# A hybrid encoder block on one core: the plan of its long convolution rearranged, and a second buffer for turned chunks

## The chip, the cores and the metric

The kernel runs on one core of a Trainium2 chip (one launch, one program). The metric is the device time of one execution in microseconds. Times are medians of several executions; the profile is of one more execution of the same program.

## What is computed

One block for 256 tokens of width 2048, in float32:

```python
proj = h @ w_in
q, k, v, r, af, ab, hy_u, gate_logits = split(proj)
y_gla = gla(q, k, v, r, af, ab)              # gated linear attention, both directions
uc = short_conv(hy_u)                        # 3 taps and a bias per channel
z, x1, x2 = split(uc, 3)
for o, gate in enumerate((x1, x2)):          # a long convolution by FFT, twice
    z = gate * (irfft(rfft(z, 2 * L) * filt_f[:, o])[:L] + skip[o] * z)
g = sigmoid(gate_logits)
merged = g[0] * (y_gla @ w_gla_o) + g[1] * (z @ w_hy_o)
h = layernorm(ALPHA * h + merged @ w_out)
ff = relu(h @ w_ff1) ** 2 @ w_ff2
out = layernorm(ALPHA * h + ff)
```

## The kernel before

**Weights.** All large weights lie in HBM as blocks of 128 x 2048 float32 values (1 MB). `fetch` (L100) loads one block through SyncE's queue into one of three `raw` buffers and splits each half of it into a high and a low part: ScalarE casts the half to `whi` (L92), and VectorE subtracts (`wlo`, L93). There are three buffers of each, so a cast can begin only when TensorE has finished with the half three before it. `token_group` (L242) multiplies four blocks with both token halves: `token_half` (L224) does 12 matmuls of 512 columns per half block, three for each pair of a block row and a token half (L233 to L235). Its two results lie in two of the four main PSUM buffers; they must be read out before the next group but one begins. Two blocks are always loaded ahead of the one that is being multiplied.

**The stretch around the change.** For each of four units of 512 channels, four token groups run one after the other: the three inputs v, x1 and x2 of the convolution (tiles `uv`, `ux`, L942), and one group of the attention's output projection (`go`, L903). Beside them the rest of the convolution has to be done for the unit. This work is put between the weight halves by a planner. `work(at, cost, fn)` (L119) files a step with a due time; `on_time` (L123) does the same for a step that must stay in program order. `fill` (L126) is called once after each half block, which is one tick. It adds 1.75 us to a budget (of which at most 0.875 us is carried over) and takes steps strictly by due time until the first one is not yet due or costs more than is left:

```python
budget[0] = min(budget[0], PACE / 2) + PACE
while filling:
    e = min(filling, key=lambda e: e[:2])
    if not every and (e[0] > tick[0] or e[2] > budget[0]):
        break
```

A unit has 32 ticks; its start is the tick at which its v group has been filed. `keep_in_program_order` fixes the order of the steps that it is given among each other; where the rest goes on its engine is chosen when the program is built.

**The steps of one unit.** `short_conv` (L765) makes each of the three inputs: six products of a PSUM result with a row of taps (L773: two centre taps into the input's tile `cv` or `cx`, two "past" taps and two "ahead" taps into side tiles, the upper half of `conv_sb` or `shift`), the bias (L777), and then `shift` (L779): four accumulating DMAs in GpSimd's queue (L787) that add the side tiles into the input, moved by one token, and the load of the next input's taps in SyncE's queue (L760). Then, twice (order 0 with v and x1, order 1 with the result and x2):

- `load`: the filter's spectrum from HBM into `Tl` through GpSimd's queue (L802); one buffer
- `input`: ScalarE casts the whole input to `zh` (L809); `low`: VectorE's remainder `zl` (L813)
- `fwd`: 12 matmuls of the forward transform into four PSUM buffers of the side pool, which has four (`Ze`, `Zo`), and two copies to `pb` (L824)
- `sum`, `mul`, `join`, `fold`, `split`: VectorE (L830, L842, L846, L853, L863), with a ScalarE cast in each split (L862)
- `inv`: 12 matmuls into two side PSUM buffers (`yp`); `gate`: two VectorE products with x1 or x2 (L876)

After order 1, `turn`: `hy_turn` (L878) transposes a chunk of 256 channels on TensorE into a side PSUM buffer (`yT`), ScalarE copies it to `yo` (L889), and a step filed two ticks later stores `yo` to HBM through GpSimd's queue (`yd`, L893). The tile `yo` has one buffer, the tag `sum` of the pool `base`. Two chunks come from each unit; the last two of the eight are split directly and not stored. After the last unit, while four groups of gate logits (`g`) run, the six stored chunks are loaded again (L955), and the projection `ho` reads all eight.

The due times stand in `PLAN` (L908), counted from the unit's start, and in the loop at L940: v's taps at 0, x1's at 8, x2's at 16. Most of a unit's order 1 falls into the ticks of the next unit.

Of the kernel before, what the change touches and what calls it, by code (L numbers as in the profile page):

```python
# [9 lines left out]
F32 = mybir.dt.float32  # L10
# [6 lines left out]
P = 128  # L17
D = 2048
L = 256
# [30 lines left out]
def block_kernel(  # L50
# [28 lines left out]
    base = ctx.enter_context(tc.tile_pool(name="base", bufs=1))  # L79
# [8 lines left out]
    def psum_side(name):  # L88
        return sdp.tile([P, 512], F32, tag="sd", name=name)

    def split_hi_lo(hi, lo, src):
        return (nc.scalar.copy(hi, src),  # L92
                nc.vector.tensor_tensor(lo, src, hi.bitcast(F32), op=ALU.subtract))  # L93
# [25 lines left out]
    def work(at, cost, fn):  # L119
        clock[1] += 1  # L120
        filling.append((at, clock[1], cost, fn))

    def on_time(at, cost, fn):  # L123
        work(at, cost, lambda: tc.keep_in_program_order(fn()))
# [12 lines left out]
    def weight_half(n, h):  # L137
        return (wp.tile([P, D // 2], F32R, tag="whi", bufs=3, name=f"whi{n}_{h}"),
                wp.tile([P, D // 2], F32R, tag="wlo", bufs=3, name=f"wlo{n}_{h}"))
# [149 lines left out]
    with tc.tile_pool(name="xp", bufs=1) as xp, tc.tile_pool(name="xq", bufs=1) as xq:  # L289
# [25 lines left out]
        for i in range(3):  # L315
            t = weight_half(-1, i)
# [194 lines left out]
    for i in range(2 * NCH):  # L511
        c, o = divmod(i, 2)
        n = 4 + (i * 21) // 15
# [236 lines left out]
    hp = hstk.enter_context(tc.tile_pool(name="hp", bufs=1))  # L750
# [8 lines left out]
    def load_taps(i):  # L759
        return nc.sync.dma_start(conv_sb[:, 0:2].rearrange("p a b -> p (a b)"),  # L760
                                 conv_rows[i:i + 1, :].broadcast_to([P, 2048]))
# [3 lines left out]
    def short_conv(at, pss, i, tag, name):  # L765
        past, ahead = shifted[i % 2][:, 0:NT], shifted[i % 2][:, NT:]

        def place():
            cst[tag, i // 3] = hp.tile([P, NT, 512], F32, tag=tag, name=name)

        def tap(j, tb):
            y = cst[tag, i // 3]
            return TT((past, y, ahead)[j][:, tb], pss[tb], taps[:, j], op=ALU.mult)  # L773

        def bias():
            y = cst[tag, i // 3]
            return TT(y, y, taps[:, 3:4].broadcast_to([P, NT, 512]), op=ALU.add)  # L777

        def shift():  # L779
            y = cst[tag, i // 3]  # L780
            for dst, src in (
                (y[:, 1], past[:, 0]),
                (y[1:P, 0], past[0:P - 1, 1]),
                (y[:, 0], ahead[:, 1]),
                (y[0:P - 1, 1], ahead[1:P, 0]),
            ):
                nc.gpsimd.dma_start(dst, src, accum_op=ALU.add)  # L787
            if i + 1 < 12:
                tc.keep_in_program_order(load_taps(i + 1))

        work(at, 0.0, place)
        for n, (j, tb) in enumerate((j, tb) for j in (1, 0, 2) for tb in range(NT)):
            on_time(at + 0.4 * n, 0.68, lambda j=j, tb=tb: tap(j, tb))
        on_time(at + 2.4, 1.2, bias)
        work(at + 2.4, 0.0, shift)

    def halves_of(ap):
# [2 lines left out]
    def hy_load(s, o):  # L800
        t = hp.tile([P, 2, 1024], F32, tag="Tl", name=f"Tl{s}{o}")
        nc.gpsimd.dma_start(t, T_dram[(s, o)].rearrange("p r h s c -> p r (h s c)"))  # L802
        cst[("T", s, o)] = t

    def hy_input(s, o):
        src = cst.pop(("v", s)) if o == 0 else cst[("x1", s)]
        z = tuple(hp.tile([P, NT, 512], F32R, tag=t, name=f"{t}{s}{o}") for t in ("zh", "zl"))
        cst[("z", s, o)] = z + (src,)
        tc.keep_in_program_order(nc.scalar.copy(z[0], src))  # L809

    def hy_low(s, o):
        zh, zl, src = cst[("z", s, o)]
        return TT(zl, src, zh.bitcast(F32), op=ALU.subtract)  # L813

    def hy_fwd(s, o):
        zh, zl, _ = cst.pop(("z", s, o))
        x = hp.tile([P, 2, 2, 2, CW], F32, tag="X", name=f"X{s}{o}")
        b = hp.tile([P, 2, 1024], F32, tag="pb", name=f"pb{s}{o}")
        odds = []
        for ri in range(2):  # L820
            even, odd = psum_side(f"Ze{s}{o}{ri}"), psum_side(f"Zo{s}{o}{ri}")
            for ps, i in ((even, 0), (odd, 1)):
                mm3(ps, dfth[:, 2 * i + ri], dftl[:, 2 * i + ri], zh[:, i], zl[:, i], True, True, hold=True)
            nc.scalar.copy(b[:, ri, 0:512], even)  # L824
            odds.append(odd)
        cst[("X", s, o)] = (x, b, odds)

    def hy_sum(s, o, ri, k):
        x, b, odds = cst[("X", s, o)]
        return TT(x[:, ri, :, k], halves_of(b[:, ri, 0:512]), halves_of(odds[ri]), op=(ALU.add, ALU.subtract)[k])  # L830

    def hy_mul(s, o, ri, k):
        x, b, _ = cst[("X", s, o)]
        t = cst[("T", s, o)]
        x = x.rearrange("p r h k c -> p r (h k c)")
        if ri == 0:
            if k == 0:
                cst[("a", s, o)] = hp.tile([P, 2, 1024], F32, tag="pa", name=f"pa{s}{o}")
            b = cst[("a", s, o)]
        else:  # L840
            x = x[:, ::-1]
        return TT(b[:, k], x[:, k], t[:, ri], op=ALU.mult)  # L842
# [31 lines left out]
    def hy_gate(s, o, i):  # L874
        g = cst[(("x1", "x2")[o], s)]
        return TT(g[:, i], cst.pop(("py", s, o, i)), g[:, i], op=ALU.mult)  # L876

    def hy_turn(c, zf):  # L878
        def run():
            pt = psum_side(f"yT{c}")  # L880
            for cc in range(2):
                for tb in range(NT):
                    nc.tensor.transpose(pt[:, cc * L + tb * P:cc * L + (tb + 1) * P], zf[:, tb, cc * P:(cc + 1) * P], ident)
            pt = pt.rearrange("p (a b) -> p a b", a=2)
            if c >= NCH - 2:
                split_hi_lo(yhT[:, 2 * c:2 * c + 2, 0], yhT[:, 2 * c:2 * c + 2, 1], pt)
                return
            yo = base.tile([P, 2, L], F32, tag="sum", name=f"yo{c}")
            nc.scalar.copy(yo, pt)  # L889

            def keep():
                yd = drp.tile([P, 2, L], F32, tag=f"yd{c}", name=f"yd{c}")
                nc.gpsimd.dma_start(yd, yo)  # L893
                yh_dram[c] = yd
            work(tick[0] + 2, 0.0, keep)
        return run
# [3 lines left out]
    def gla_o_group(at):  # L900
# [4 lines left out]
        for tb in range(NT):  # L905
            on_time(at, 0.68, lambda tb=tb: TT(mg[:, tb], mg[:, tb], pss[tb], op=ALU.mult))

    PLAN = (  # L908
        dict(load=3, input=9, low=9.5, fwd=10.4, sum=11.5, mul=12, join=15, fold=17.6, split=19.5, inv=20.5, gate=22),
        dict(load=16.5, input=22.5, low=23, fwd=26, sum=26.5, mul=28, join=30.5, fold=35, split=36.5, inv=37,  # L910
             gate=41, turn=43),
    )

    def unit_steps(at, s):
        for o, plan in enumerate(PLAN):
            t = {k: at + v for k, v in plan.items()}
            work(t["load"], 0.0, lambda o=o: hy_load(s, o))
            work(t["input"], 0.0, lambda o=o: hy_input(s, o))
            on_time(t["low"], 1.2, lambda o=o: hy_low(s, o))
            work(t["fwd"], 0.0, lambda o=o: hy_fwd(s, o))  # L920
            for ri in range(2):
                for k in range(2):
                    on_time(t["sum"], 0.68, lambda o=o, ri=ri, k=k: hy_sum(s, o, ri, k))
            for ri in range(2):
                for k in range(2):
                    on_time(t["mul"], 1.2, lambda o=o, ri=ri, k=k: hy_mul(s, o, ri, k))
            for step, fn in (("join", hy_join), ("fold", hy_fold), ("split", hy_split)):
                for k in range(2):
                    on_time(t[step], 1.2, lambda o=o, k=k, fn=fn: fn(s, o, k))
            work(t["inv"], 0.0, lambda o=o: hy_inv(s, o))  # L930
            for i in range(2):
                on_time(t["gate"], 0.68, lambda o=o, i=i: hy_gate(s, o, i))
            if o:
                for i in range(2):
                    work(t["turn"] + 2 * i, 0.0, lambda i=i: hy_turn(
                        2 * s + i, cst[("x2", s)][:, :, i * CW:(i + 1) * CW])())

    load_taps(0)
    paced[0] = True
    for s in range(NCH // 2):  # L940
        for n, (k, d) in {"v": (0, 0), "x1": (1, 8), "x2": (2, 16)}.items():
            pss = token_group(xT, f"u{n}{s}")  # L942
            if k == 0:
                t0 = tick[0]
                unit_steps(t0, s)
            short_conv(t0 + d, pss, 3 * s + k, n, f"c{n}{s}")
        gla_o_group(t0 + 24)
# [615 lines left out]
    with tc.high_priority(), tc.issue_after(done.ins):  # L1563
# [3 lines left out]
        y, t, v, rs = (ep.tile([P, 1], F32, tag=f"fin{i}", name=f"fin{i}") for i in range(4))  # L1567
# [160 lines left out]
```

## Time and profile before

| | us |
|---|---|
| median of 3 runs | 1802.42 |
| lowest and highest of them | 1802.08, 1803.63 |
| the profiled execution | 1799.02 |
| its span, first to last instruction | 1797.1 |
| VectorE busy in the span | 1460.3 |
| ScalarE busy in the span | 1047.8 |
| first matmul of `uv` to first matmul of `g` after the units | 429.8 to 839.2 |

In the rows of the profile, PE is TensorE, PEld its weight load, DVE VectorE, ACT ScalarE, POOL GpSimd and SP SyncE. A row in order of time gives the start in us from the span's start, the duration in us, the engine, the line, the operation, the tile written and the tiles read, and the count; in brackets stands how long the engine was idle before it and what ended that. A row of waits gives the waiting engine, tile and line, what it waited for, and then the sum in us, the number of waits and the longest. In a row of stretches, the number in brackets counts the instructions that were at work in the stretch; the granted clock, the share of the DMA engines and their GB/s follow.

### The profile page before, as it was taken

The page shows a single profiled execution, that of the slowest core. Times are in us where ns is not written, and L with a number is a line of the kernel's source. Part 1 is how long each engine was busy: PE and PEld are TensorE (multiplying, and loading weights), DVE is VectorE, ACT ScalarE, POOL GpSimd, SP SyncE. Part 2 cuts the span into 40 slices and gives each one's busy share as a digit, 9 for nine tenths or more (in the row PEclk, how much of TensorE's full clock was granted, in tenths as well). Part 3 has the DMA queues.
Part 4 walks back from the last instruction along what each step waited for, and adds up shares of the span by engine and source line. Part 5 has one row for each costly group of instructions (what it writes and reads, how often), then busy time and mean ns, then how long its engine had stood idle before and what let it go on. Part 6 is the DMA issues. An engine that isn't in the chain of part 4 may idle for free.

```text
span 1797.1 us, 23574 instructions
## 1 busy us (share of the span) xinstructions
PE 1775.9 (99%) x8739; PEld 1497.7 (83%) x8739; DVE 1460.3 (81%) x1899; ACT 1047.8 (58%) x1446; POOL 186.7 (10%) x243
## 2 busy tenths in 40 slices
PE   9999999999999999999999999999999999999998
PEld 7888888888788788787888889988888888888886
DVE  6689887785588788787855557789999999999998
ACT  6587876785344343443544435666666666666663
POOL 1001111000011101111000000011111111111110
PEclk9999999999999999999999999999999999999999
DMA  8677888545688778778655574588888888887864
GB/s 329 224 265 264 278 256 260 172 156 210 212 280 253 232 233 254 229 256 244 221 181 193 212 289 173 200 257 245 254 264 244 243 273 244 267 252 242 262 216 166
DMA packets 87315, 427.13 MB, mean 238 GB/s; under 512 B 9816, under 2 KB 14312, under 8 KB 45600
## 3 DMA queue, kind: packets, MB, share of 16 engines
q1 hardware_dynamic: 47664, 336.35, 51.1%
q0 software_dynamic: 30560, 67.38, 18.1%
q10 hardware_dynamic: 8976, 21.89, 3.4%
q8 instruction: 68, 1.11, 0.2%
q14 instruction: 47, 0.39, 0.1%
HBM read 382.12 MB, written 12.06 MB: 219 GB/s over the span
## 4 chain that ended last, share of the span: by engine, by line
PE 50%; DVE 3%; DMA 0%; issue 0%; ACT 0%; DVEq 0%
PE f L176 12%; PE f L180 6%; PE w L1360 5%; PE w L1359 5%; PE w L1361 5%; PE g L233 2%; PE g L234 2%; PE ho L234 2%; PE ho L233 2%; PE g L235 2%; PE ho L235 2%; PE wo L234 1%; PE wo L235 1%; PE wo L233 1%; PE f L209 1%; DVE zr L1217 1%
## 5 line engine op out<-in xcount | busy, mean ns | idle before, releaser
L93 DVE TENSOR_TENSOR wlo<-raw,whi 128x1024 fp32r<-128x1024 f32 x360 | 438.9, 1223 | 198.5 <-ACT whi L92 195.8
L92 ACT CAST whi<-raw 128x1024 fp32r<-128x1024 f32 x360 | 376.9, 1054 | 366.9 <-PE ux L235 93.1
L176 PE MATMUL f<-hT,whi 128*128 128x512 f32 x984 | 243.9, 391 | 0.0
L176 PEld LDWEIGHTS f<-hT,whi 128*128 128x128 f32 x984 | 180.8, 188 | 34.9
L1217 DVE TENSOR_TENSOR wlo<-fraw,whi 128x1024 fp32r<-128x1024 f32 x112 | 136.9, 1222 | 14.2 <-ACT whi L1220 10.9
L180 PEld LDWEIGHTS f<-hT,wlo 128*128 128x128 f32 x984 | 126.2, 191 | 4.8
L180 PE MATMUL f<-hT,wlo 128*128 128x256 f32 x984 | 127.7, 283 | 0.0
L1220 ACT CAST whi<-ring 128x1024 fp32r<-128x1024 f32 x56 | 59.0, 1054 | 114.3 <-DVE ring L1217 114.3
L1280 POOL DMA_DIRECT2D ring<-wblk x56 | 48.6, 868 | 728.7 <-DVE ring L1217 722.3
L1220 ACT CAST whi<-fraw 128x1024 fp32r<-128x1024 f32 x112 | 117.7, 1051 | 0.0
L1220 ACT CAST b_h<-ring 128x1024 fp32r<-128x1024 f32 x112 | 87.9, 834 | 22.7 <-PE w L1361 21.1
L234 PE MATMUL ux<-wlo,xT 128*128 128x512 f32 x256 | 100.5, 392 | 0.5 <-DVE wlo L93 0.5
L234 PE MATMUL g<-wlo,xT 128*128 128x512 f32 x256 | 100.3, 392 | 0.0
L235 PE MATMUL ux<-whi,xT 128*128 128x512 f32 x256 | 100.3, 392 | 0.0
L235 PE MATMUL g<-whi,xT 128*128 128x512 f32 x256 | 100.0, 391 | 0.0
L233 PE MATMUL g<-whi,xT 128*128 128x512 f32 x256 | 92.5, 391 | 0.6 <-DVE shift L773 0.6
L233 PE MATMUL ux<-whi,xT 128*128 128x512 f32 x256 | 90.7, 390 | 2.4 <-ACT whi L92 2.4
L1217 DVE TENSOR_TENSOR ring<-ring 128x512 f32<-128x512 f32 x112 | 77.2, 689 | 1.9
L1217 DVE TENSOR_TENSOR b_l<-ring,b_h 128x1024 fp32r<-128x1024 f32 x56 | 68.4, 1221 | 8.6 <-ACT b_h L1220 8.5
L1217 DVE TENSOR_TENSOR wlo<-ring,whi 128x1024 fp32r<-128x1024 f32 x56 | 68.6, 1225 | 2.8 <-ACT whi L1220 1.0
L1217 DVE TENSOR_TENSOR fa<-ring,fa 128x1024 fp32r<-128x1024 f32 x56 | 68.3, 1219 | 0.0
L1281 POOL DMA_DIRECT2D ring<-ring x56 | 65.7, 1174 | 0.1
(529 smaller groups left out, 4268.0 us busy)
## 6 DMA issues: line engine op xcount, KB each, us to landing
raw<-wblk SPq DMA_DIRECT2D x188, 1024.0 KB, 5.0
fraw<-wblk SPq DMA_DIRECT2D x56, 1024.0 KB, 4.9
ring<-wblk SPq DMA_DIRECT2D x56, 1024.0 KB, 6.9
ring<-wblk POOLq DMA_DIRECT2D x56, 256.0 KB, 4.4
ring<-ring POOLq DMA_DIRECT2D x56, 256.0 KB, 5.1
conv_sb<-conv_rows SPq DMA_DIRECT2D x12, 1024.0 KB, 5.8
w<-w4s ACTq DMA_DIRECT2D x16, 512.0 KB, 5.2
Td<-T POOLq DMA_DIRECT2D x32, 256.0 KB, 4.8
```

Source lines behind the costliest of these rows:

```text
L92: return (nc.scalar.copy(hi, src), nc.vector.tensor_tensor(lo, src, hi.bitcast(F32), op=ALU.subtract))
L93: nc.vector.tensor_tensor(lo, src, hi.bitcast(F32), op=ALU.subtract))
L176: MM(ps[:, :, ts], hi[:, js], act[:, kt, :, ts], start=(kt == 0 and opens), stop=(kt == KT - 1))
L180: MM(ps[:, 0, ts], lo[:, js], act[:, kt, 0, ts], start=False, stop=False)
L233: order(MM(pss[tb], sh, wh, start=(kt == ends[0]), stop=False))
L234: order(MM(pss[tb], sh, wl, start=False, stop=False))
L235: order(MM(pss[tb], sl, wh, start=False, stop=(kt == ends[1])))
L1217: return pin(nc.vector.tensor_tensor(dst, a, b, op=op))
L1220: return pin(nc.scalar.copy(hi, src))
L1359: pin(MM(ps, sh, wh, start=(p == begin), stop=False))
L1360: MM(ps, sh, wl, start=False, stop=False)
L1361: pin(MM(ps, sl, wh, start=False, stop=(p == end - 1)))
```

## The change

Four things change. In `short_conv` the bias is filed at 0.6 behind the two centre taps, ahead of the four outer ones, instead of at 2.4 behind all six. In `PLAN` nearly all due times move: the input cast of order 0 from 9 to 11.6, its remainder and transform after it, the products spread by 0.7 a step, joins from 15 to 19, and in order 1 the load from 16.5 to 20 and the input cast from 22.5 to 24.6. The third input's taps are due at 16.2 instead of 16, which is now ahead of the first order's joins. The copies of turned chunks alternate between the pool `base` and the pool `hp`, so there are two buffers, and the second turn is due one tick behind the first and not two.

```diff
@@ short_conv
         for n, (j, tb) in enumerate((j, tb) for j in (1, 0, 2) for tb in range(NT)):
+            if n == 2:
+                on_time(at + 0.6, 1.2, bias)
             on_time(at + 0.4 * n, 0.68, lambda j=j, tb=tb: tap(j, tb))
-        on_time(at + 2.4, 1.2, bias)
         work(at + 2.4, 0.0, shift)
@@ hy_turn
-            yo = base.tile([P, 2, L], F32, tag="sum", name=f"yo{c}")
+            yo = (hp if c % 2 else base).tile([P, 2, L], F32, tag="sum", name=f"yo{c}")
@@ PLAN
-        dict(load=3, input=9, low=9.5, fwd=10.4, sum=11.5, mul=12, join=15, fold=17.6, split=19.5, inv=20.5, gate=22),
-        dict(load=16.5, input=22.5, low=23, fwd=26, sum=26.5, mul=28, join=30.5, fold=35, split=36.5, inv=37,
-             gate=41, turn=43),
+        dict(load=3, input=11.6, low=12, fwd=12.2, sum=13.6, mul=14, join=19, fold=20, split=21, inv=21.5, gate=24.2),
+        dict(load=20, input=24.6, low=25, fwd=25.5, sum=28, mul=29.5, join=35, fold=36.5, split=38, inv=38.5,
+             gate=41, turn=42.5),
@@ unit_steps
-                    on_time(t["mul"], 1.2, lambda o=o, ri=ri, k=k: hy_mul(s, o, ri, k))
+                    on_time(t["mul"] + 1.4 * ri + 0.7 * k, 1.2, lambda o=o, ri=ri, k=k: hy_mul(s, o, ri, k))
-                    work(t["turn"] + 2 * i, 0.0, lambda i=i: hy_turn(
+                    work(t["turn"] + i, 0.0, lambda i=i: hy_turn(
                         2 * s + i, cst[("x2", s)][:, :, i * CW:(i + 1) * CW])())
@@ the loop over units
-        for n, (k, d) in {"v": (0, 0), "x1": (1, 8), "x2": (2, 16)}.items():
+        for n, (k, d) in {"v": (0, 0), "x1": (1, 8), "x2": (2, 16.2)}.items():
```

## The prediction

> **What bounds the kernel now.** The page first: which engine is full, and how full.
>
> ```profile
> span 1797.1 us, 23574 instructions
> PE 1775.9 (99%) x8739; PEld 1497.7 (83%) x8739; DVE 1460.3 (81%) x1899; ACT 1047.8 (58%) x1446; POOL 186.7 (10%) x243
> ```
>
> TensorE has work at nearly every moment of the 1797.1 us, so an edit elsewhere can gain only what TensorE loses now. Second, the waits of 400 to 960 us, the stretch that holds the part of the program which the plan orders:
>
> ```profile
> ACT yo L889 <- DMA yd<-yo: 24.6, 3, 8.7
> ...
> DVE cx L876 <- PE yp L374: 17.5, 8, 4.2
> ...
> PE go L233 <- ACT whi L92: 8.2, 3, 3.3
> ...
> PE ux L233 <- ACT whi L92: 2.4, 1, 2.4
> ...
> PE g L233 <- DVE shift L773: 0.6, 1, 0.6
> ...
> PE uv L233 <- DVE conv_sb L773: 0.3, 1, 0.3
> ```
>
> Four times TensorE waits for a weight cast (whi): three times in a go group, once in a ux group. Behind that stand two waits of ScalarE for a DMA: the copy of a turned chunk (yo) waits for the store of the chunk before it, and the input cast (zh) waits for the adding DMAs of the convolution. Third, ScalarE in order of time, at the first and the second of the four places, with one undisturbed weight cast ahead of them:
>
> ```profile
> 457.39 1.05 ACT L92 CAST whi<-raw 128x1024 fp32r<-128x1024 f32 x1 [1.67 <-PE ux L235]
> ...
> 487.63 1.04 ACT L809 CAST zh<-cv 128x1024 fp32r<-128x1024 f32 x1 [7.42 <-DMA cv<-conv_sb]
> 488.58 1.99 ACT L92 CAST whi<-raw 128x1024 fp32r<-128x1024 f32 x2
> ...
> 617.22 0.58 ACT L889 COPY yo<-yT 128x512 f32<-128x512 f32 x1 [8.71 <-DMA yd<-yo]
> ```
>
> The weight casts queue behind the waiting instruction and come out in a row afterwards (x2). Undisturbed, one comes each 1.05 + 1.67 = 2.72 us: that is a tick of the plan. Fourth, TensorE around the first place and the last:
>
> ```profile
> 486.65 0.39 PE L234 MATMUL ux<-wlo,xT 128*128 128x512 f32 x1
> 486.88 0.39 PE L235 MATMUL ux<-whi,xT 128*128 128x512 f32 x1
> 489.67 0.73 PE L233 MATMUL ux<-whi,xT 128*128 128x512 f32 x2 [2.40 <-ACT whi L92]
> 490.93 0.79 PE L234 MATMUL ux<-wlo,xT 128*128 128x512 f32 x1 [0.53 <-DVE wlo L93]
> 491.52 0.63 PE L235 MATMUL ux<-whi,xT 128*128 128x512 f32 x1
> 491.95 0.63 PE L234 MATMUL ux<-wlo,xT 128*128 128x512 f32 x1
> ...
> 828.01 0.78 PE L233 MATMUL go<-whi,yg 128*128 128x512 f32 x2 [1.82 <-ACT whi L92]
> 829.27 0.80 PE L234 MATMUL go<-wlo,yg 128*128 128x512 f32 x1 [0.48 <-DVE wlo L93]
> 829.86 0.63 PE L235 MATMUL go<-whi,yg 128*128 128x512 f32 x1
> ...
> 839.17 0.47 PE L233 MATMUL g<-whi,xT 128*128 128x512 f32 x1 [0.64 <-DVE shift L773]
> ```
>
> Starts lie 0.23 us apart before the wait (486.65, 486.88) and 0.43 us apart after it (491.52, 491.95). So a wait costs more than its length: matmuls run slower for a few us behind it. The whole price is therefore read from counts. A 20 us stretch without a wait, then one around each of the four places:
>
> ```profile
> core 0: us, PE busy (x), PEclk, DMA share, GB/s
> 540.00:560.00 20.00, 20.00 (x90) 1.00 0.72 244
> 480.00:500.00 20.00, 17.07 (x69) 0.91 0.56 172
> 612.00:632.00 20.00, 15.89 (x61) 0.91 0.65 215
> 718.00:738.00 20.00, 16.07 (x61) 0.91 0.64 214
> 822.00:842.00 20.00, 17.06 (x67) 0.91 0.68 216
> ```
>
> 90 matmuls fit where nothing waits; 21, 29, 29 and 23 are missing at the four places, and the granted clock is 0.91 in each. A matmul of this shape takes 0.227 us (starts of 486.65 to 486.88, and 20 us over the 88 or so that start in the first stretch), so the places lose 4.8 + 6.6 + 6.6 + 5.2 = 23.1 us. The last three stretches also hold the small waits for a released PSUM buffer (0.64 and its like, rows g and uv). No other stretch of this part of the program holds a listed wait: 23.1 us is all that the plan can give.
>
> **The change part by part.**
>
> *Bias ahead of the outer taps.* VectorE does the same six products and one sum per input; only their order changes, so its work costs nothing more. The adding DMAs go out earlier. Before:
>
> ```profile
> 459.62 1.28 DVE L773 TENSOR_TENSOR cv<-uv,conv_sb 128x512 f32<-128x512 f32 x2
> 460.81 0.68 DVE L773 TENSOR_TENSOR conv_sb<-uv,conv_sb 128x512 f32<-128x512 f32 x1
> ...
> 462.54 1.88 DVE L773 TENSOR_TENSOR conv_sb<-uv,conv_sb 128x512 f32<-128x512 f32 x3
> 464.34 1.22 DVE L93 TENSOR_TENSOR wlo<-raw,whi 128x1024 fp32r<-128x1024 f32 x1
> 465.47 1.23 DVE L777 TENSOR_TENSOR cv<-cv,conv_sb 128x1024 f32<-128x1024 f32 x1
> ...
> 467.01 1.82 POOL L787 DMA_DIRECT2D cv<-conv_sb  x2 [35.77 <-DVE cv L777]
> ...
> 479.95 0.88 POOL L787 DMA_DIRECT2D cv<-conv_sb  x1 [2.77 <-DMA cv<-conv_sb]
> ```
>
> The first add waits for the bias, the last of the seven steps, which ends at 466.7. In the new order it needs two centre taps (1.2 us, 459.62 to 460.81), the bias and one weight remainder (1.13 each, 464.34 to 465.47) and two "past" taps (1.2): 459.62 + 4.7 = 464.3, so the chain starts 2.4 us earlier. It took from 467.01 to the release of zh at 487.63, 20.6 us; shifted it lands at 485.2.
>
> *Input cast from 9 to 11.6 (first order).* Going through the planner's rule tick by tick (strictly by due time, 1.75 us of budget per half block), the cast sits behind weight cast 9 of the unit before the change and behind weight cast 12 after it. Weight cast 1 is the row of 457.39, so weight cast 12 starts at 457.39 + 11 x 2.72 = 487.3 and the input cast at 488.3: 3.1 us after the adds have landed. The 7.42 us wait goes, and with it the 4.8 us of the first place. If the cover of 3.1 us were missed, more slack follows: weight cast 10 was due at 481.9, started at 488.58, 6.7 us late, and TensorE waited 2.40 of that, so 4.3 us of ScalarE's lateness cost nothing. What is late next: in the later units the cast is at tick 12 instead of 10 and has two ticks (5.4 us) and the earlier adds for itself.
>
> *Two buffers for turned chunks, and turns one tick apart.* Before, the planner puts the first copy at tick 12 of the next unit; its store and the second copy, both held up behind the products of the second frequency step, come together at tick 17, and the one buffer makes the second copy wait for the store to land (8.71 us, three times). After, both turns sit at tick 12, both stores at tick 15, and each copy's buffer was last used a unit, 32 ticks, earlier. The three waits go: 6.6 + 6.6 + 5.2 us. At tick 12 ScalarE then has a weight cast, two copies and the input cast, 1.05 + 2 x 0.58 + 1.04 = 3.25 us in 2.72: 0.5 us late, inside the 4.3.
>
> *Third input's taps ahead of joins and folds.* They sit at ticks 18 to 20 instead of 19 to 22, before TensorE needs their PSUM buffers at the next group but one. The waits of 0.3 to 0.6 us go; they are in the 23.1 already.
>
> *Later sums, products, joins, folds, splits and gates.* The same instructions. The first order's gates fall at tick 26 (24 and 25 before), the second order's at 10 and 11 of the next unit (10 before); in the last unit at 41, as before, with the turns at 43 and 44 instead of 43 and 45, while the product that reads them (ho) begins 56 ticks after the unit's start. So the end of the stretch doesn't move, and cost is nothing.
>
> *Load of the second order's filter, from tick 18 to 23.* POOL's queue has the third input's four adds ahead of it now: they hold the queue from 467.01 to 480.8, 13.8 us, five ticks from tick 20, so the load goes out by tick 25.
>
> ```profile
> L802 POOL DMA_DIRECT2D Tl<-Td x8: 541/564/890, 430.7 to 827.9; - x8
> ...
> DMA to landing us min/median/max: 5.1/5.8/12.7
> ```
>
> It lands 5.8 us later (12.7 at most), tick 27 to 30, and the first product that reads it is at tick 30, with 24 transform matmuls (5.4 us) between that belong to no tick. It stays hidden; if that cover goes, VectorE stands, and behind it the weight remainders. The other queue entries that move wait for nothing new: the third input's step also puts the next taps' load into SP's queue, at tick 20 instead of 22 or 23, and the stores of turned chunks go into POOL's at tick 15 behind the second input's adds, read again only by the reloads after the last unit.
>
> *What the trace doesn't show* is how the new order meshes where TensorE's transform, the gates and the turns follow each other closely: one small wait per unit, at the turns, is possible. The nearest small waits are 0.3 (uv) and 0.6 (g); the far bound is a wait like the four of now, 5.8 us on average (23.1 / 4); a gain is excluded, since nothing beyond the 23.1 is lost. I take 0.3 for each of three units, 0.9 us, the row of a buffer released a little late.
>
> *Sum.* 23.1 - 0.9 = 22.2 us. The profiled execution took 1799.02 us, 1.9 beyond its span, and would take 1776.8; the median of the runs is 1802.42, 3.4 above it, and would be 1780.2.
>
> [...]
>
> **The rivals.** (a) *The slow stretch isn't the wait's.* At the first and last places the waits themselves are 2.40 + 0.53 and 1.82 + 0.48 + 0.64, 5.9 us of the 4.8 + 5.2; if the other 4.1 have another cause and stay, the gain is 18.1 and the time 1784.3. For it: these two gaps are the short ones. Against it: the slow matmuls stand right behind each gap and in no other of the counted stretches. [...]
>
> (b) *The cast still comes before the adds land.* The adds' speed depends on what else is moving. If tick 12 is early by more than 3.1 + 4.3 us, the first place stays (4.8) or all four units get one (5.8 each): 1785.0 to 1803.4. Against it: the four stops of now have three yo and only one zh in front of them.
>
> (c) *The turns take the side PSUM buffers.* Two turned chunks hold two of four side buffers right ahead of the transform, which needs four. If its matmuls wait for both copies and the cast between (2.2 us, plus about 2.4 of slow matmuls as at the first place), three units lose 4.6 in place of the 0.3: 13.8 us, time 1793.1. Against it: the copies stand ahead of the cast on ScalarE.
>
> (d) *Slower: the gates become the wait.* VectorE stands at the gates for the inverse transform already, 17.5 us over eight waits, 2.2 each, with the weight remainders behind it and the second input cast behind the gate on ScalarE. The first order's gates move next to each other at tick 26 with that cast at the same tick. If the inverse's second half comes 2.1 us or more later than now, the lateness (2.2 + 2.1) passes the 4.3 us of slack, and a place like the four (5.8) appears at each of eight gates: 46.4 - 23.1 = 23.3 lost, 1825.7. From four places on nothing is gained, from five on it is slower. Against it: the split now has a tick of its own ahead of the gates, where before both shared one.
>
> **How the numbers follow.** The forecast gets 0.70, (a) 0.04, (b) 0.12, (c) 0.06, (d) 0.08. About 0.2% (3.6 us) is what a measurement of this kernel can tell from no change. Faster: 0.70 + 0.04 + 0.09 of (b) + 0.05 of (c) = 0.88. Same: 0.03 of (b), 0.01 of (c), 0.01 of (d) = 0.05. Slower: 0.07. The range starts at 1776, the profiled execution less the whole 23.1, and goes to 1792, two of the four places left or the like in new places; (d), most of (c) and the dear end of (b) are outside.
>
> **What would show it.** Right: zh and yo without a wait for a DMA of over a us; 90 or so matmuls in each 20 us of the stretch, clock 1.00; whi no longer among TensorE's releasers there; the stretch from the first uv to the first g2 matmul some 22 us shorter. Wrong: a go, ux or uv matmul waiting for whi or wlo (then the instruction ahead of that cast on ScalarE or VectorE names the rival: zh (b), the gate (d)), or Ze waiting for a copy (c).

## The result and the profile after

The changed kernel took 1775.76 us (median of 4 runs, 1774.91 to 1777.13) against 1802.25 us for the kernel before (4 runs, 1797.46 to 1803.63). The ratio is 0.9858, 95% interval 0.9839 to 0.9878: 1.4% faster. The profiled execution took 1776.26 us, 22.8 us less than the one of before. The median lies 0.2 us under the 1776 us at which the predicted range begins.

The first two lines of the page after:

```profile
span 1774.5 us, 23593 instructions
PE 1766.4 (100%) x8739; PEld 1494.0 (84%) x8739; DVE 1460.1 (82%) x1899; ACT 1048.9 (59%) x1446; POOL 186.5 (11%) x243
```

The instructions of every compute engine are the same in number and VectorE's work is the same to 0.2 us; what is gone is TensorE's waits and its slow matmuls. All waits of TensorE of the whole execution, in the kernel after (engine and line that waited, what for; us in total, times, longest):

```profile
PE warm L305 <- DVE ones_sb L367: 1.5, 1, 1.5
PE open L329 <- ACT whi-1_2_134 L341: 1.0, 1, 1.0
PE w L234 <- DVE wr L93: 0.3, 1, 0.3
```

None of them lies in the four units. The same stretches as in the prediction, after (us, TensorE busy with the number of matmuls, granted clock, DMA share, GB/s):

```profile
480.00:500.00 20.00, 20.00 (x90) 1.00 0.91 284
540.00:560.00 20.00, 20.00 (x90) 1.00 0.47 167
612.00:632.00 20.00, 20.00 (x90) 1.00 0.97 322
718.00:738.00 20.00, 20.00 (x90) 1.00 0.79 258
822.00:842.00 20.00, 20.00 (x90) 1.00 0.64 194
```

The 102 missing matmuls are back, at a clock of 1.00. The stretch from the first uv matmul to the first g matmul after the units (the prediction's g2) took 409.3 us before and 386.5 us after. It is shown before and after, with TensorE alone:

```profile
429.80:839.20 409.40, 395.50 (x1720) 0.98 0.77 246
430.40:816.90 386.50, 386.50 (x1720) 1.00 0.80 261
```

That is 22.8 us less (409.3 less 386.5, from first start to first start), the whole gain of the profiled execution. About 13.9 us of it was idle time (409.4 less 395.5) and 9.0 us slow matmuls (395.5 less 386.5); after, TensorE is busy from end to end. ScalarE in order of time in the kernel after, at the input cast of the first unit and at the turns of the second:

```profile
487.84 1.06 ACT L92 CAST whi<-raw 128x1024 fp32r<-128x1024 f32 x1 [1.66 <-PE ux L235]
488.80 1.05 ACT L810 CAST zh<-cv 128x1024 fp32r<-128x1024 f32 x1
...
590.92 1.08 ACT L890 COPY yo<-yT 128x512 f32<-128x512 f32 x2 [1.36 <-PE yT L884]
591.88 1.06 ACT L810 CAST zh<-cv 128x1024 fp32r<-128x1024 f32 x1
```

Neither zh nor yo waits for a DMA any more: where the brackets said 7.42 and 8.71 us, there is none now, or it names TensorE's transposes (yT).

### The profile page after: what moved, and what is told of

Read it like the earlier page. It is cut to its first block, busy times and chain, and to the rows that moved or that the text cites. A ratio compares the mean times of both kernels' runs of the same rounds, so it can differ in the third digit from the quotient of the medians.

```text
span 1774.5 us, 23593 instructions
## 1 busy us (share of the span) xinstructions
PE 1766.4 (100%) x8739; PEld 1494.0 (84%) x8739; DVE 1460.1 (82%) x1899; ACT 1048.9 (59%) x1446; POOL 186.5 (11%) x243
## 4 chain that ended last, share of the span: by engine, by line
PE 96%; DVE 2%; DMA 1%; issue 0%; ACT 0%; SPq 0%; DVEq 0%
PE f L176 13%; PE f L180 7%; PE w L1360 5%; PE w L1361 5%; PE w L1362 5%; PE g L234 3%; PE g L235 3%; PE g L233 3%; PE ux L234 3%; PE ux L235 3%; PE ux L233 3%; PE k L176 2%; PE r L234 2%; PE r L235 2%; PE r L233 2%; PE v L235 2%
```

## The experiments

The theory: TensorE loses time only where ScalarE waits for a DMA in front of a weight cast. Three of these waits belong to the one buffer of turned chunks and one to the first unit's input cast. ScalarE may be some 4.3 us late before it costs anything. The main rival: the new order of VectorE's steps is what freed TensorE. Ratios are to the kernel before on the same chip.

**Two buffers alone.** In the kernel before:

```diff
-            yo = base.tile([P, 2, L], F32, tag="sum", name=f"yo{c}")
+            yo = (hp if c % 2 else base).tile([P, 2, L], F32, tag="sum", name=f"yo{c}")
```

> The kernel before with one edit: the copies of turned chunks alternate between two buffers. Theory (each ScalarE wait for a DMA is what stops TensorE; three belong to the one buffer, one to the input cast): the three places in the go groups go, 18.4 us less the 1.9 us of small waits for PSUM that stand in the same stretches and stay, so 16.5 us gained, time near 1785.8, ratio 0.991; the place at the first unit's input cast stays, with some 21 matmuls missing in its 20 us. Rival (the new order of VectorE's steps is what frees TensorE, the buffer alone turns one wait into another): under 6 us gained, ratio 0.997 or more, and go matmuls still wait for whi.

Measured: 1781.64 us (1779.34 to 1782.54), ratio 0.9891 (0.9860 to 0.9922). Waits of TensorE in it:

```profile
PE ux L233 <- ACT whi L92: 3.0, 1, 3.0
...
PE ux L234 <- DVE wlo L93: 0.5, 1, 0.5
```

The 20 us around the first unit's place:

```profile
480.00:500.00 20.00, 16.96 (x61) 0.83 0.58 170
```

The theory holds: of the four places only the first unit's is left. (The wait of 0.5 us is a new one, in the third unit, where zh waited 4.7 us for the adds.) The two profiled executions lie 16.5 us apart (1799.02 and 1782.54), as expected, but by two differences that nearly cancel. The small waits for PSUM (uv and g for the third input's taps) went too, although those taps stand where they stood. They were an aftermath: VectorE came out of each yo stop late, and the taps with it (in the second unit they begin at 622.20 us before and at 616.57 here). And the first unit's place got dearer, with 29 matmuls missing instead of 21. The medians lie 19.7 us apart; why that is more than the profiles show is taken up below.

**One buffer in the changed plan.** In the changed kernel:

```diff
-            yo = (hp if c % 2 else base).tile([P, 2, L], F32, tag="sum", name=f"yo{c}")
+            yo = base.tile([P, 2, L], F32, tag="sum", name=f"yo{c}")
```

> The changed kernel with one buffer for turned chunks again; all due times as changed. Theory: the second copy follows the first at the same tick, while the first's store is filed three ticks later, so three places come back, each at least as dear as now (6 us), 18 us or more: ratio to before 0.996 or higher, perhaps above 1. Rival (the plan does it, the buffer is spare): within 4 us of the changed kernel, ratio under 0.988.

Measured: 1814.11 us (1813.13 to 1814.91), ratio 1.0076 (1.0049 to 1.0102): slower than before. Its waits in 400 to 960 us, then ScalarE and TensorE in order of time at the second unit:

```profile
PE Ze L370 <- DVE zl L814: 30.5, 3, 10.7
...
ACT yo L890 <- DMA yd<-yo: 20.0, 3, 7.2
```

```profile
601.94 0.59 ACT L890 COPY yo<-yT 128x512 f32<-128x512 f32 x1 [6.10 <-DMA yd<-yo]
602.42 1.05 ACT L810 CAST zh<-cv 128x1024 fp32r<-128x1024 f32 x1
```

```profile
604.78 0.79 PE L370 MATMUL Ze<-zl,dfth 128*128 128x512 f32 x1 [9.57 <-DVE zl L814]
605.38 0.63 PE L373 MATMUL Ze<-zh,dfth 128*128 128x512 f32 x1
605.80 0.63 PE L374 MATMUL Ze<-zh,dftl 128*128 128x512 f32 x1
```

The second copy waits for the first store; this time the input cast is behind it, and TensorE stops at the transform (Ze) that needs it, three times for about 10 us. So without the second buffer the rest of the change is worth less than nothing: it puts the two turns closer together and needs that buffer.

**Bias late, or cast early, or both.** Three variants of the changed kernel: the bias behind all six taps again; order 0's cast due at 9 again; both.

```diff
-            if n == 2:
-                on_time(at + 0.6, 1.2, bias)
             on_time(at + 0.4 * n, 0.68, lambda j=j, tb=tb: tap(j, tb))
+        on_time(at + 2.4, 1.2, bias)
```

> The changed kernel with the bias back behind all six taps. Theory (the cast's later due time is enough): the adds land some 2.4 us later, still about when the cast is due at tick 12, and ScalarE's 4.3 us of slack takes the rest: within 2 us of the changed kernel, ratio to before 0.985 to 0.987, no ux, uv or go matmul waiting. Rival (the bias ahead is needed): the first unit's place comes back, 4.8 us, ratio 0.988 or more, with a zh wait of over 4 us.

```diff
-        dict(load=3, input=11.6, low=12, fwd=12.2, ...
+        dict(load=3, input=9, low=9.5, fwd=10.4, ...
```

> The changed kernel with order 0's cast, remainder and transform due at 9, 9.5 and 10.4 again; bias ahead, two buffers. Theory (slack of 4.3 us): zh waits 2 to 4 us for the adds and no matmul waits: 1775 to 1777.5. Rival (the later due time is what frees the first unit): 4 us or more above the changed kernel, with a ux wait.

> The changed kernel with both undone that concern the adds: cast due at 9, bias behind all taps; only the buffers, the turns and the later rest of the plan stay. Theory: the first unit's place comes back alone, one ux wait of 2 to 3 us and slow matmuls behind it, 4.8 us: 1779.5 to 1782. Rival (the rest of the plan hides the adds anyway): 1777.5 or less, no ux wait.

Measured: bias late 1775.52 us (1775.08 to 1778.26), ratio 0.9865 (0.9838 to 0.9891); cast at 9 1775.10 us (1774.78 to 1775.95), ratio 0.9861 (0.9844 to 0.9878); both 1782.61 us (1781.36 to 1787.64), ratio 0.9907 (0.9885 to 0.9929). With both, 0.6 us above the upper end expected, TensorE waits at the first unit as before; the row of its waits:

```profile
PE ux L233 <- ACT whi L92: 2.4, 1, 2.4
```

So, with the rest of the changed plan, either of the two edits cures the first unit's place, and neither is needed beside the other. With the cast due at 9 the expected 2 to 4 us wait of zh was a miss: the planner, with the bias taking budget earlier, takes the cast at tick 10, and the adds had all but landed. ScalarE at that place with the cast at 9 and the bias ahead:

```profile
483.96 1.05 ACT L810 CAST zh<-cv 128x1024 fp32r<-128x1024 f32 x1 [0.54 <-DMA cv<-conv_sb]
```

**How late ScalarE may be.** Both of the above undone, and the cast due at 10 or at 8 instead of 9:

```diff
-        dict(load=3, input=9, low=9.5, fwd=10.4, ...
+        dict(load=3, input=10, low=10.5, fwd=11.2, ...      # and: input=8, low=8.5, fwd=9.4
```

> Cast due at 9 and bias late in the changed kernel (1782.6 us, one ux wait of 2.4 us) with the cast due one tick later, at 10, remainder 10.5, transform 11.2. Theory (ScalarE may be late by 4.3 us for nothing): zh still waits some 4.7 us for the adds, the weight cast behind it is 4.0 us late and no matmul waits: 1774.5 to 1777.5. Rival (each wait of that length on ScalarE costs its length less a little): a ux wait of a us or more, 1779 or above.

> The same with the cast due one tick earlier than 9, at 8, remainder 8.5, transform 9.4. Theory (slack 4.3 us, then one for one, and a slow stretch of about 2.3 us behind each stop, whatever its length): zh in the first unit waits 10.1 us, TensorE 5.1 and 2.3 more; in the later units zh waits some 8 to 9 us and TensorE up to 4 and 2.3 each: 1783 to 1801. Rival (only the first unit ever stops, as in the kernel before): 1785 or less, one ux wait.

Measured: at 10, 1777.24 us (1776.76 to 1785.42), ratio 0.9888 (0.9863 to 0.9912); at 8, 1784.97 us (1781.01 to 1790.68), ratio 0.9922 (0.9899 to 0.9946). ScalarE at the first unit, with the cast at 10, at 9 and at 8:

```profile
482.49 1.06 ACT L92 CAST whi<-raw 128x1024 fp32r<-128x1024 f32 x1 [1.67 <-PE ux L235]
487.82 1.05 ACT L809 CAST zh<-cv 128x1024 fp32r<-128x1024 f32 x1 [4.28 <-DMA cv<-conv_sb]
488.78 2.94 ACT L92 CAST whi<-raw 128x1024 fp32r<-128x1024 f32 x3
```

```profile
478.98 1.05 ACT L92 CAST whi<-raw 128x1024 fp32r<-128x1024 f32 x1 [1.67 <-PE ux L235]
487.43 1.04 ACT L809 CAST zh<-cv 128x1024 fp32r<-128x1024 f32 x1 [7.40 <-DMA cv<-conv_sb]
488.38 2.94 ACT L92 CAST whi<-raw 128x1024 fp32r<-128x1024 f32 x3
```

```profile
479.15 1.05 ACT L92 CAST whi<-raw 128x1024 fp32r<-128x1024 f32 x1 [1.67 <-PE ux L235]
488.27 1.04 ACT L809 CAST zh<-cv 128x1024 fp32r<-128x1024 f32 x1 [8.07 <-DMA cv<-conv_sb]
489.22 2.93 ACT L92 CAST whi<-raw 128x1024 fp32r<-128x1024 f32 x3
```

A weight cast is due 2.72 us after the one before it. The casts behind zh come at 488.78 instead of 485.21, at 488.38 instead of 481.70, and at 489.22 instead of 481.87: 3.6, 6.7 and 7.4 us late. TensorE waited 0, 2.4 and 3.0 us for them. The slack is 4.3 us, and beyond it TensorE waits one us for each us late; the slow matmuls behind the wait come on top. Near the edge it isn't safe: one of the four runs with the cast at 10 took 1785.4 us, and no profile of it was taken. At 8, zh went out behind the same weight cast as at 9 and waited 8.1 us, not 10.1. In the profiled execution the later units stop too, at the transform; the waits of TensorE:

```profile
PE Ze L370 <- DVE zl L813: 5.8, 3, 3.2
PE ux L233 <- ACT whi L92: 3.0, 1, 3.0
```

This profile is of the slowest of the four runs (1790.68 us), and its stretch of the four units is 14.7 us longer than in the changed kernel. The other three runs took 1781.0 to 1785.8 us, 5 to 10 us more than the changed kernel, so they can't have had all these stops in full. The median alone doesn't separate the theory from its rival; that the later units can stop is shown by this one execution.

**The rest of the plan.** Two smaller versions of the change, both with two buffers: bias ahead on the old due times; and the bias late, with order 0's cast at 11.6 and its sums and products shifted behind it.

```diff
+            if n == 2:
+                on_time(at + 0.6, 1.2, bias)
             on_time(at + 0.4 * n, 0.68, lambda j=j, tb=tb: tap(j, tb))
-        on_time(at + 2.4, 1.2, bias)
```

> The kernel before with two buffers for turned chunks and the bias ahead of the outer taps; the due times as before, so the cast at 9. Theory (ScalarE may be 4.3 us late for nothing): the adds land some 2.5 to 3 us earlier than with two buffers alone, the weight cast behind the input cast is 3.4 us late instead of 6.7, and TensorE doesn't wait for it: 1775 to 1777.5, 5 us under two buffers alone. Rival (the cast has to stand behind the adds): a ux wait stays at the first unit, 1779 or more.

```diff
-        dict(load=3, input=9, low=9.5, fwd=10.4, sum=11.5, mul=12, join=15, ...
+        dict(load=3, input=11.6, low=12, fwd=12.2, sum=12.6, mul=13, join=15, ...
```

> The kernel before with two buffers and order 0's cast at 11.6, remainder at 12, transform at 12.2, and, since they follow it, sums at 12.6 and products at 13; nothing else moved (bias last, turns two ticks apart, order 1 and joins as before). Theory (two waits of ScalarE were the whole loss): as fast as the changed kernel, 1774 to 1778, no matmul of the units waits. Rival (the joins, the third input's taps and order 1 have to move too, for the PSUM waits): 1778 or more, with uv or g waiting for the products with the taps.

Measured: 1788.74 us (1787.04 to 1789.46), ratio 0.9935 (0.9917 to 0.9952), and 1782.48 us (1781.73 to 1782.93), ratio 0.9900 (0.9880 to 0.9920). Both missed the theory's numbers, and the first is worse than the buffers alone. TensorE's waits in the two, one fence each, and in the second also VectorE in order of time at the first gates:

```profile
PE uv L233 <- DVE conv_sb L773: 3.1, 2, 2.3
PE g L233 <- DVE shift L773: 2.3, 1, 2.3
PE uv L233 <- DVE shift L773: 2.3, 1, 2.3
```

```profile
PE uv L233 <- ACT whi L92: 1.2, 1, 1.2
PE uv L234 <- DVE wlo L93: 1.0, 1, 1.0
...
PE uv L233 <- DVE conv_sb L773: 0.8, 1, 0.8
PE g L233 <- DVE shift L773: 0.8, 1, 0.8
PE uv L233 <- DVE shift L773: 0.7, 1, 0.7
```

```profile
535.36 0.69 DVE L876 TENSOR_TENSOR cx<-yp,cx 128x512 f32<-128x512 f32 x1 [2.48 <-PE yp L374]
535.97 1.22 DVE L93 TENSOR_TENSOR wlo<-raw,whi 128x1024 fp32r<-128x1024 f32 x1
```

No stop at the first unit's ux group in either. In its place the next unit's v group (or, after the last unit, the first g group) waits for PSUM buffers that the third input's taps still read. The first row of the second fence names a weight cast, but that cast came in its turn (518.05, then 520.81), and the matmul went out 0.15 us after a tap ended, as in the other three units; it is likely the same wait. The row for wlo is another one: VectorE stood 2.5 us at a gate, and the weight remainder came out behind it.

By the planner's rule the last of these taps comes at tick 23 in the first of the two kernels, with the bias ahead of it: one tick later than before, stuck behind order 0's joins and folds. In the second it comes at 22, as before; why it is late there was not tried. (VectorE's sums wait 20.9 us for the forward transform there, 8.5 us with two buffers alone.) The next run starts from the first of the two and moves only order 0's joins and what follows them:

```diff
-        ... join=15, fold=17.6, split=19.5, inv=20.5, gate=22),
+        ... join=19, fold=20, split=21, inv=21.5, gate=24.2),
```

> Two buffers and bias ahead on the old due times (1788.7 us, with four waits of 0.9 to 2.3 us of uv and g for the third input's taps), and in it only order 0's joins at 19, folds at 20, splits at 21, inverse at 21.5 and gates at 24.2. Theory (the third input's last tap is stuck behind order 0's joins and folds; now it comes at tick 20 instead of 23, ahead of them): those waits go, 1774 to 1778. Rival (the bias ahead itself costs, or the products behind it): 1783 or more, the waits stay.

In this kernel order 1's cast (22.5) comes ahead of order 0's gate, so order 1 works on the ungated x1; the instructions are the same in kind and number. Measured: 1775.64 us (1774.89 to 1776.59), ratio 0.9869 (0.9852 to 0.9885), and no matmul of the units waits. The theory holds: 13 us of the 1788.74 hung on the place of the joins and of the four steps behind them.

**The kernel before once more.**

> The kernel before, unchanged, for its own spread: its four runs so far went from 1797.5 to 1803.6 us, those of the changed kernel from 1774.9 to 1777.1. Theory (the four waits end with a DMA's landing, whose time varies): the matmuls missing in the four places differ from the first profile's 102, and the time with them, by 0.227 us each. Rival (the spread comes from elsewhere): 102 missing again within 5, and the span differs in another part of the program.

Measured: 1801.25 us (10 runs, 1797.87 to 1803.55), ratio 1.0002 (0.9987 to 1.0016). The stretches of its profile:

```profile
480.00:500.00 20.00, 17.49 (x70) 0.91 0.57 177
612.00:632.00 20.00, 16.15 (x69) 1.00 0.68 226
718.00:738.00 20.00, 14.87 (x57) 0.91 0.58 207
822.00:842.00 20.00, 16.48 (x64) 0.91 0.67 220
```

20, 21, 33 and 26 are missing, 100 in all. The single places differ from the first profile (29 and 29 at the middle two there), the sum does not. The stretch from the first uv to the first g matmul is 409.0 us, against 409.3; the 1.5 us by which the span is longer lie ahead of it and behind it. By the expectation that is the rival's result: this pair of profiles doesn't show that the spread of the kernel before comes from the four places.

## Why the prediction was right, and where it was off

**The loss.** It put all that the plan could give at 23.1 us, from the missing matmuls, and the profiled execution at 1776.8 us. The four units lost 22.8 us of length, and the execution took 1776.26. Of the 0.9 us that it kept for new small waits nothing appeared.

**The failed step is the last one,** from the profiled execution to the median: "3.4 above it, and would be 1780.2". That 3.4 us was carried over, but it belongs to the kernel before, and in good part to the one execution of it that was profiled: in the second profile of before (1800.36) it is 0.9 us to the median of its runs. After, the median (1775.76) lies 0.5 us under the profiled execution, and the four runs span 2.2 us where ten runs of the kernel before span 5.7. So the gain of the medians, 26.5 us, is 3.7 us larger than that of the two profiles. Why the other runs of before are longer stays open in part. Their mean granted clock was 0.993 to 0.996; over 1797 us that is 7 to 13 us' worth of lost rate, and the two runs with the lowest clock (0.993, 0.994) took 1801.89 and 1803.55 us, those with 0.996 between 1797.87 and 1801.46 and those with 0.995 1801.15 and 1803.14. Of thirteen more runs of before on that chip the two with the highest clock (0.998, 0.999) were the shortest, 1794.24 and 1794.05 us; the other eleven, at 0.993 to 0.997, took 1798.49 to 1804.26 in no clear order. After, no run is under 0.999. That points to the stops, but no profile of a long run was taken, and the second profile of before lost the same as the first.

**Bias and cast.** The first add was expected at 464.3 us and went out at 464.74; the cast was expected at 488.3 and began at 488.80. The adds were to land at 485.2; in the run with the cast at 9 the cast that waited for them began at 483.96. That the two edits together remove the first place was right; whether both are needed was not asked, and the runs show that one is enough.

**Two buffers.** The largest part, as predicted: 19.7 us between the medians and 16.5 us between the profiled executions with this edit alone (18.4 us were put on it), and a slower kernel than before when it alone is taken back.

**The third input's taps** were costed as removing waits of 0.3 to 0.6 us. That was a wrong cause: with two buffers alone the waits go without it. What their place ahead of the joins does is another thing, which the prediction missed: it keeps the bias's earlier place from making those waits 2.3 us long. The later joins are enough for that: in the last experiment on the plan the third input's taps are still due at 16.

**The rivals.** (a), that the slow matmuls have another cause, is out: none of the counted stretches has fewer than 90 matmuls now that the waits are gone. (b) is what happens with both edits undone, one place, as it said for the smallest case: the stretch of the four units is 4.9 us longer than in the changed kernel, where 4.8 were expected. (The time for it, 1785.0 against 1782.61 measured, stood on the same median of 1780.2.) That the adds' speed depends on what else is moving shows in the first profile of before: twelve times two adds of like size go out within 0.6 us, and each time the second took longer to land, by 1.4 to 4.4 us (9.1 and 12.1 us in the first unit). (c) did not come: no Ze matmul waits. The like of it comes when the cast is held up behind the second copy (10 us each). (d) did not come either: VectorE's waits at the gates grew by 1.1 us only. The row of before was 17.5 (eight waits, the longest 4.2); after:

```profile
DVE cx L877 <- PE yp L374: 18.6, 9, 2.7
```

A small case of it is the wait for wlo, 1.0 us, in the smaller version above.

**A faster version** than the changed kernel wasn't found: two variants (bias late, cast at 9) are as fast within their spread, and in the four units TensorE has no wait left to remove. The run with only the joins later is as fast too, but it leaves out order 0's gate from what order 1 reads, so it is no version of this kernel.

## What to carry to other kernels

On an engine that feeds the bound one, look for the instruction that waits for a DMA and ask what is queued behind it: its cost begins only beyond the slack of the buffers that it feeds (here 4.3 us); from there on the wait grew about one for one (6.7 us late cost 2.4 us, 7.4 us cost 3.0), and a slow stretch of the bound engine may come on top (1.5 to 3.3 us where it was measured here). A due time moved to cure one wait moves what shares its budget: check who is now last at the next buffer, here the taps behind the joins. When a change removes stops, take its time from the profiled execution less the loss; the distance from one profiled execution to the median of a few runs was no property that the new kernel kept here.

## What the runs showed of the hardware that was not expected

After many a stop TensorE's matmuls run at 0.43 us a start instead of 0.23 for a while, but in these runs the length of the stop alone decides neither whether, nor how long. With bias ahead on the old due times the next group starts three times after equal waits of 2.3 us. TensorE there, at the second and third of them:

```profile
725.80 0.47 PE L233 MATMUL uv<-whi,xT 128*128 128x512 f32 x1 [2.28 <-DVE conv_sb L773]
726.11 0.39 PE L234 MATMUL uv<-wlo,xT 128*128 128x512 f32 x1
726.34 0.39 PE L235 MATMUL uv<-whi,xT 128*128 128x512 f32 x1
...
827.47 0.77 PE L233 MATMUL g<-whi,xT 128*128 128x512 f32 x1 [2.28 <-DVE shift L773]
828.03 0.63 PE L234 MATMUL g<-wlo,xT 128*128 128x512 f32 x1
828.46 0.63 PE L235 MATMUL g<-whi,xT 128*128 128x512 f32 x1
```

The first goes on at full rate, the other at about half. The slow stretch added 1.5 us there (73 matmuls in the 20 us around it, 79 around the first), 2.2 to 2.5 us after the stops of 1.8 to 3.3 us in the kernel before (with a second wait of 0.5 us in each), and 2.3 to 3.0 us after the stops of about 10 us with one buffer (what the starts are further apart than 0.227 us, summed over the stretch). After equal waits of 3.0 us it added 3.3 us with two buffers alone and 1.7 us with the cast at 8. In the second profile of before, a wait of 1.9 us (uv for shift) was followed by matmuls at full rate (clock 1.00 from 612 to 632 us), while the wait of 1.82 us in the first was followed by slow ones (0.63 us instead of 0.39). After the five waits of 0.7 to 1.2 us in the smaller version with the bias late TensorE went on at full rate (its mean granted clock is 1.000). What decides between the two isn't shown by any run.
